# Where the loaded weights begin within a line of the on-chip memory: a two-layer transformer on one TensorE

## The chip, the cores and the metric

The kernel runs on one core of a Trainium2 chip. It has five engines that work side by side and wait for each other through semaphores: TensorE (PE in the profile; PEld is its weight load), VectorE (DVE), ScalarE (ACT), GpSimd (POOL) and SyncE (SP, which here issues the weight transfers). The metric is the device time of one launch in microseconds (us).

## What is computed

Two layers run one after the other on 256 tokens of width 2048. The first layer has a modulation (`adaln`), neighbourhood attention over 16 heads, and a feed-forward part with a short convolution. The second layer has 8 heads of a chunked recurrence (`mlstm`) and 16 heads of causal attention. The operations that matter here are the large products:

```python
q, k, v = split(h @ w_qkv)                          # 2048 x 6144
x = x + g1 * (attention(q, k, v) @ w_o)             # 2048 x 2048
gate, up = split(dwconv3(hf @ w_up))                # 2048 x 11008
x = x + g2 * ((silu(gate) * up) @ w_down)           # 5504 x 2048
proj = rms_norm(x) @ w_in_2                         # 2048 x 15440
y_a = (sigmoid(o_a) * h_a * silu(z_a)) @ w_a        # 2048 x 2048
y_b = (o_b * silu(z_b)) @ w_b                       # 2048 x 2048
out = x + (sigmoid(g_a) * y_a + sigmoid(g_b) * y_b) @ w_out
```

## The kernel before, in words

**Split numbers.** Each float32 operand of a product is split in two parts of a reduced type (float32r): `hi` holds the leading bits and `lo` the rest. A product is then hi·hi + hi·lo + lo·hi.

**Weights.** All weights are cut into units (`Unit`, line 179) and run in one fixed list. The planner in `run_units` (line 389) is plain Python that runs while the program is built: it keeps a clock of its own and writes each engine's instructions down in an order. SP brings a unit of 1 MB into a `raw` tile. `emit_prep` (line 343) splits each half of a unit: ACT casts `raw` into a `whi` tile and DVE subtracts to make a `wlo` tile, of 1024 columns each. There are five buffers of each.

**Two ways to multiply.** In `GemmX` (line 491) the activations are loaded into the array and the weights move through it. In `GemmW` (line 476) it is the other way round: 128 weight columns are loaded and held, and the activations move. There, the activations of one k-chunk stand side by side as 256 `hi` and 256 `lo` columns, so that one product with `whi` moves 512 columns and one with `wlo` moves the 256 `hi` columns. This is called a pair below: 512 columns, then 256, each with a weight load of its own. Every `GemmW` comes out of `pair_units` (line 1071). The profile names a product as out<-moving,loaded: `bank<-hf,whi` moves `hf` and has `whi` loaded.

**Which products are pairs.** The second half of the attention output (`o`), the whole feed-forward part (`hf`, `hid`), nearly all of the second layer's projections (`h2`, which the profile shows as `h`, since it leaves numbers out) and its three output products (`ya`, `ob`, `yp`).

**Addresses.** A tile of the program begins at a fixed byte in each partition of the on-chip memory. Lines 534 and 535 put in two small tiles (64 bytes on the left, 32 on the right) that do nothing but shift what comes after. As the program is laid out, `raw` begins at a multiple of 128 bytes, and `whi`, `wlo`, `h`, `o`, `hf`, `hid`, `h2`, `ya`, `ob`, `yp`, `latq` and `latkv` all begin 64 bytes past one. The steps within them (128 columns, 256, 512) are multiples of 128 bytes, so every weight load and every moving read of those tiles begins 64 bytes past a multiple of 128.

**The gate ring.** In the second layer's attention the gates `z` (16 tiles of 128x256, one a head) are computed ahead of the head that uses them: `mla_z` (line 1722) takes a buffer of `zring` (profile: `bz`) as soon as a gate's product is done, and `mla_attn` (line 1862) gives it back after the head's output has been multiplied by it (profile: `obF<-bank,bz`). The work list has two gates (heads 2g+2 and 2g+3), then the projections of heads 2g and 2g+1. If no buffer is idle, `need` (line 230) writes down pending steps of other heads, in the order of their due times, until one is. The main list stands still meanwhile, and PE runs its instructions in the order written.

**gone.** A small tile of 8x256 that `misc` (line 1417) uses once while it computes the recurrence's gates. The ring `E` (one buffer) is used by the recurrence's heads, which start after that.

Of the kernel before, what the change touches and what calls it, by code (L numbers as in the profile page):

```python
# [12 lines left out]
F32 = mybir.dt.float32  # L13
F32R = mybir.dt.float32r
# [96 lines left out]
class Bank:  # L111
    def __init__(self, owner, i):
        self.owner, self.i, self.busy, self.tfree = owner, i, False, 0.0
# [65 lines left out]
class Unit:  # L179
    def __init__(self, src, kt, cols, body=None, pre=None, post=None, raw=None):  # L180
        self.src, self.kt, self.cols = src, kt, cols
        self.body, self.pre, self.post, self.raw = body, pre, post, raw
        h = (kt + 1) // 2
        self.subs = [(0, h), (h, kt - h)] if kt > 1 else [(0, 1)]
        if raw is not None:
            self.subs = [(0, kt)]


class Kern:
# [153 lines left out]
    def emit_prep(self):  # L343
        u, s = self.preps[self.np]
        self.np += 1
        k0, nk = u.subs[s]
        self.ct = max(self.now, u.ready)
        if u.raw is not None:
            u.raw(u.view)
        else:  # L350
            n = nk * u.cols
            hi = self.p_w.tile([128, 1024], F32R, tag="whi", name="whi")
            lo = self.p_w.tile([128, 1024], F32R, tag="wlo", name="wlo")
            src = u.tile[:, k0 * u.cols:k0 * u.cols + n]
            self.A.copy(out=hi[:, 0:n], in_=src)
            self.nsplit += 1

            def rest():
                self.V.tensor_sub(out=lo[:, 0:n], in0=src, in1=hi[:, 0:n])
                u.parts[s] = tuple(x[:, 0:n].rearrange("p (k c) -> p k c", k=nk) for x in (hi, lo))  # L360
                u.at[s] = self.ct
                if s == len(u.subs) - 1:
                    self.next_dma(u)
            self.at(max(0.0, self.ct - self.now), rest)
            return
        self.next_dma(u)
# [161 lines left out]
class Model(Kern):  # L528
# [542 lines left out]
    def pair_units(self, w, K, c0, xs, evac, need=None, pre=None, nb=2, j0=0, nj=2):  # L1071

        us = []
        for p in range(0, nj, nb):
            def done(j, out, b, last, p=p):
                self.spawn(evac(j0 + p + j, out, b), 0.2 + 0.4 * j)
            g = GemmW(self, K, nb, xs, done, need)
            us += self.block_units(w, K, c0 + 128 * p, 128 * nb, g, kt=16 // nb)
        us[0].pre = pre
        return us  # L1080

# [232 lines left out]
    def c_begin(self):  # L1314
        sums = self.stats_sums()
        self.L.pop("hid")
        self.R.pop("x2")
        p = self.L.push("ya")
        self.sgring = Ring(self, p, "sga", [128, 256], F32, 8)
        self.ya = p.tile([128, KD, 512], F32R, name="ya")  # L1320
        self.yaH, self.yaL = self.ya[:, :, 0:256], self.ya[:, :, 256:512]
        p = self.R.push("cp")
        self.cg = {x: p.tile([128, 2, 64], F32, name="cg" + x) for x in "qk"}
        self.sg = {x: p.tile([128, 2, 64], F32, name="sg" + x) for x in "qk"}
        self.krt = p.tile([128, 2, 64], F32, name="krt")
        self.sskr = p.tile([128, 32], F32, name="sskr")[:, 0:2]
        r = self.r2 = p.tile([128, 256], F32, name="r2")
        self.r2c = p.tile([128, 32], F32, name="r2c")[:, 0:2]
        p = self.R.push("ml")
        self.p_ml = p  # L1330
        self.qring = Ring(self, p, "mq", [128, 2, 256], F32R, 3)
        self.kring = Ring(self, p, "mk", [128, 2, 256], F32R, 3)
        self.vring = Ring(self, p, "mv", [128, 2, 2, 288], F32R, 3)
        self.gring = Ring(self, p, "G", [128, 2, 256], F32, 3)
        self.cring = Ring(self, p, "mct", [128, 256], F32, 3)
        self.soring = Ring(self, p, "so", [128, 256], F32, 4)
        self.ering = Ring(self, p, "E", [128, 384], F32, 1)
        self.wring = Ring(self, p, "W", [128, 2, 384], F32R, 1)
        self.haring = Ring(self, p, "ha", [128, 256], F32, 2)
        self.tring = Ring(self, p, "T", [128, 512], F32, 1)  # L1340
        self.fring = Ring(self, p, "fold2", [128, 256], F32, 2)
        self.krx2 = p.tile([128, 256], F32, name="krx2")
        for nm in ("gi", "gz", "ga", "gb", "gc", "gone"):
            setattr(self, nm, p.tile([8, 256], F32, name=nm))
        self.acol = p.tile([128, 2, 8], F32, name="acol")
        self.fcol = p.tile([128, 2, 8], F32, name="fcol")
        for v in self.vring.tiles:
            for x in range(2):
                one = self.con("one") if x == 0 else self.con("tri0")[:, 0:1]
                self.V.tensor_copy(out=v[:, x, :, 256:258], in_=one.unsqueeze(1).to_broadcast([128, 2, 2]))  # L1350
        self.q, self.k, self.v, self.Gt = {}, {}, {}, {}
        self.qk_ready, self.mv_ready, self.G_ready, self.ya_ready = {}, {}, {}, set()
        self.gates_ready = self.kr_ready = self.rope_done = False
        self.c_ready = True
        yield from self.stats_end(D, sums, r, self.r2c)
        self.r_ready = True
        self.spawn(self.rope_tables(p), 1.0)
# [339 lines left out]
    def mla_begin(self):  # L1697
        self.need(lambda: self.y_stashed == 4)
        self.L.pop("ya")
        self.R.pop("y")  # L1700
        self.sgring = Ring(self, self.L.push("sgb"), "sgb", [128, 256], F32, 8)
        p = self.R.push("obf")
        self.obF = p.tile([128, KD, 256], F32, name="obF")
        p = self.R.push("mla")
        self.lat = {n: p.tile([128, 2, 4, 256], F32R, name="lat" + n) for n in ("q", "kv")}
        self.lat_ready = set()
        self.qring = Ring(self, p, "bq", [128, 2, 512], F32R, 2)
        self.kring = Ring(self, p, "bk", [128, 2, 512], F32R, 2)
        self.qrring = Ring(self, p, "bqr", [128, 2, 256], F32R, 2)
        self.krring = Ring(self, p, "bkr", [128, 2, 256], F32R, 2)  # L1710
        self.vring = Ring(self, p, "bv", [128, 2, 2, 256], F32R, 2)
        self.zring = Ring(self, p, "bz", [128, 256], F32, 6)
        self.sqring = Ring(self, p, "bsq", [128, 2, 2, 192], F32, 2)
        self.ktring = Ring(self, p, "bkt", [128, 768], F32, 1)
        self.xring = Ring(self, p, "bx", [128, 2, 2, 64], F32, 3)
        self.pring = Ring(self, p, "bp", [128, 384], F32, 2)
        self.ptring = Ring(self, p, "bpt", [128, 2, 384], F32R, 2)
        self.q, self.k, self.v, self.qr, self.kr, self.rq, self.zb = {}, {}, {}, {}, {}, {}, {}
        self.b_ready, self.ob_ready = {}, set()
        self.need(lambda: self.kr_ready)  # L1720
# [433 lines left out]
```

## Time and profile before

| | |
|---|---|
| three timed runs, us | 2603.92, 2609.01, 2610.87 (median 2609.01) |
| the profiled execution, us | 2611.98 |
| its span from first to last instruction, us | 2610.2 |
| PE busy | 2550.1 us, 98% of the span, 16038 products |
| PE weight loads busy | 2268.7 us, 87% |
| DVE, ACT, POOL busy | 71%, 54%, 9% |
| memory traffic | 522 MB, 200 GB/s |
| granted TensorE clock | 0.995 of full speed on average |

Products are pipelined, so the recorded duration of one (some 390 ns for 512 columns) is longer than the distance from its start to the next one's start. The rate is read from the starts. A row of the timeline gives start, duration, engine, line, operation, out<-in and count; the chain of waits gives start, duration and what ran, with the number of instructions.

### The profile page before, as it was taken

To read this page: it belongs to the slowest core of one execution; us is meant where nothing else is said; L and a number is where in the kernel's file an instruction comes from. 1 tells how busy PE (TensorE), PEld (TensorE's weight loads), DVE (VectorE), ACT (ScalarE), POOL (GpSimd) and SP (SyncE) were. 2 spreads that over 40 slices of the span, in tenths; PEclk is the share of its full clock that TensorE was granted. 3 is DMA by queue.
4 is the path that set the end of the run, shared out by engine and by line. 5 is a ranking of instruction groups with operands and counts; after the bars stand their busy time and mean duration, and the time that the engine had idled before them with its cause. 6 is when DMAs were issued, how large, how long until landed. Compare 5 with 4: busy or idle time off the path is not lost.

```text
span 2610.2 us, 40676 instructions
## 1 busy us (share of the span) xinstructions
PE 2550.1 (98%) x16038; PEld 2268.7 (87%) x16038; DVE 1844.4 (71%) x3027; ACT 1420.7 (54%) x2617; POOL 241.3 (9%) x263
## 2 busy tenths in 40 slices
PE   4999999999989999999999999999999999999999
PEld 2799999999978888888888888888888888888888
DVE  7987777677677888787555568677665576677664
ACT  5664444344555555555444456667554467775442
POOL 5421111111110000000000050000000000000000
PEclk9999999999999999999999999999999999999999
DMA  7876776676556666666566554554555553345553
GB/s 267 297 259 221 197 247 189 195 221 182 202 183 225 222 230 225 212 232 219 183 210 208 194 191 163 184 186 158 181 187 200 205 175 134 121 142 209 201 202 147
DMA packets 82543, 522.37 MB, mean 200 GB/s; under 512 B 9232, under 2 KB 15376, under 8 KB 23856
## 3 DMA queue, kind: packets, MB, share of 16 engines
q1 hardware_dynamic: 76656, 501.88, 54.1%
q0 software_dynamic: 5696, 17.90, 4.1%
q8 instruction: 126, 2.06, 0.3%
q14 instruction: 65, 0.53, 0.1%
HBM read 511.35 MB, written 8.39 MB: 199 GB/s over the span
## 4 chain that ended last, share of the span: by engine, by line
PE 94%; DVE 4%; ACT 1%; issue 1%; DMA 0%; SPq 0%; DVEq 0%; ACTq 0%
PE bank L256 91%; PE bank L265 2%; DVE wlo L151 2%; DVE hL L151 0%; ACT L149 0%; DMA nx<-in_ctxT_dram 0%; ACT whi L151 0%; SPq L707 0%; DVE hf L151 0%; DVE gb L151 0%; DVE mct L151 0%; DVE cc L151 0%; DVE adaC L151 0%; PE bank L608 0%; DVE acc L151 0%
## 5 line engine op out<-in xcount | busy, mean ns | idle before, releaser
L151 DVE TENSOR_TENSOR wlo<-raw,whi 128x1024 fp32r<-128x1024 f32 (+3 forms) x822 | 983.3, 1208 | 236.4 <-ACT whi L151 232.2
L151 ACT CAST whi<-raw 128x1024 fp32r<-128x1024 f32 (+3 forms) x822 | 830.5, 1021 | 422.4 <-PE bank L256 321.8
L256 PE MATMUL bank<-h,whi 128*128 128x512 f32 (+1 forms) x1696 | 593.9, 395 | 0.0
L256 PE MATMUL bank<-hf,whi 128*128 128x512 f32 x1376 | 485.0, 397 | 2.6 <-DVE hf L151 2.6
L256 PE MATMUL bank<-h,wlo 128*128 128x256 f32 x1680 | 470.7, 280 | 0.0
L256 PE MATMUL bank<-hf,wlo 128*128 128x256 f32 x1376 | 386.9, 281 | 0.0
L256 PEld LDWEIGHTS bank<-h,whi 128*128 128x128 f32 x1696 | 317.2, 188 | 71.9
L256 PE MATMUL bank<-whi,hH 128*128 128x256 f32 x1280 | 367.1, 287 | 0.0
L256 PE MATMUL bank<-whi,hL 128*128 128x256 f32 x1280 | 362.8, 283 | 2.2 <-DVE hL L151 2.2
L256 PE MATMUL bank<-wlo,hH 128*128 128x256 f32 x1280 | 362.8, 283 | 1.2 <-DVE wlo L151 1.2
L256 PEld LDWEIGHTS bank<-h,wlo 128*128 128x128 f32 x1680 | 317.4, 189 | 0.5 <-DVE wlo L151 0.3
L256 PEld LDWEIGHTS bank<-hf,whi 128*128 128x128 f32 x1376 | 259.0, 188 | 64.7 <-DVE hf L151 3.9
L256 PEld LDWEIGHTS bank<-hf,wlo 128*128 128x128 f32 x1376 | 261.1, 190 | 0.0
L256 PEld LDWEIGHTS bank<-whi,hL 128*128 128x128 f32 x1280 | 245.7, 192 | 2.5 <-DVE hL L151 2.4
L256 PEld LDWEIGHTS bank<-wlo,hH 128*128 128x128 f32 x1280 | 245.8, 192 | 2.3 <-DVE wlo L151 1.8
L256 PEld LDWEIGHTS bank<-whi,hH 128*128 128x128 f32 x1280 | 245.7, 192 | 1.0
L256 PE MATMUL bank<-hid,whi 128*128 128x512 f32 x688 | 243.1, 399 | 0.0
L256 PE MATMUL bank<-hid,wlo 128*128 128x256 f32 x688 | 193.2, 281 | 0.0
L151 DVE SCALAR_TENSOR_TENSOR acc<-raw,cs,acc 128x512 f32<-128x512 f32 x240 | 186.8, 778 | 6.8
L256 PEld LDWEIGHTS bank<-hid,whi 128*128 128x128 f32 x688 | 129.3, 188 | 32.2
L151 ACT COPY fold<-bank 128x256 f32<-128x256 f32 x118 | 43.6, 372 | 160.9 <-PE bank L256 158.2
L256 PEld LDWEIGHTS bank<-hid,wlo 128*128 128x128 f32 x688 | 130.0, 189 | 0.0
(334 smaller groups left out, 3695.7 us busy)
## 6 DMA issues: line engine op xcount, KB each, us to landing
raw<-in_w_in_dram SPq DMA_DIRECT2D x120, 1024.0 KB, 4.8
raw<-in_w_ada_dram SPq DMA_DIRECT2D x86, 1024.0 KB, 4.9
raw<-in_ffn_w_up_dram SPq DMA_DIRECT2D x86, 1024.0 KB, 4.9
raw<-in_na_w_qkv_dram SPq DMA_DIRECT2D x42, 1024.0 KB, 4.9
raw<-in_ffn_w_down_dram SPq DMA_DIRECT2D x40, 1024.0 KB, 4.9
raw<-in_na_w_o_dram SPq DMA_DIRECT2D x16, 1024.0 KB, 5.0
raw<-in_w_a_dram SPq DMA_DIRECT2D x16, 1024.0 KB, 5.0
raw<-in_w_b_dram SPq DMA_DIRECT2D x16, 1024.0 KB, 4.9
```

What stands on the lines that cost most here:

```text
L151: r = f(*a, **kw)
L256: self.T.matmul(out, lhsT, rhs, start=start, stop=stop)
L265: self.T.transpose(out, in_, self.con("id"))
```

## The change

A unit gets a flag `held`. `pair_units` sets it for all its units, that is, wherever weights are held and 512 columns move. The split tiles grow from 1024 to 1056 columns (128 bytes more, so that the next tile still begins 64 bytes past a multiple of 128), and a held unit uses columns 24 to 1047 of them. Those begin 96 bytes later: 32 bytes past a multiple of 128. Units that are not held use columns 0 to 1023 as before.

The ten split tiles take 1280 bytes a partition more. To make room, `gone` is no tile of its own but the corner of the tile `E0`, and `zring` has five buffers in place of six. Tiles after the split tiles move by 1280 bytes and those below the freed ones by 1024, both multiples of 128.

```diff
-        self.body, self.pre, self.post, self.raw = body, pre, post, raw
+        self.body, self.pre, self.post, self.raw, self.held = body, pre, post, raw, False
...
-            hi = self.p_w.tile([128, 1024], F32R, tag="whi", name="whi")
-            lo = self.p_w.tile([128, 1024], F32R, tag="wlo", name="wlo")
+            c = slice(24, 1048) if u.held else slice(0, 1024)
+            hi = self.p_w.tile([128, 1056], F32R, tag="whi", name="whi")[:, c]
+            lo = self.p_w.tile([128, 1056], F32R, tag="wlo", name="wlo")[:, c]
...
             us += self.block_units(w, K, c0 + 128 * p, 128 * nb, g, kt=16 // nb)
+        for u in us:
+            u.held = True
...
-        for nm in ("gi", "gz", "ga", "gb", "gc", "gone"):
+        for nm in ("gi", "gz", "ga", "gb", "gc"):
             setattr(self, nm, p.tile([8, 256], F32, name=nm))
+        self.gone = self.ering.tiles[0][0:8, 0:256]
...
-        self.zring = Ring(self, p, "bz", [128, 256], F32, 6)
+        self.zring = Ring(self, p, "bz", [128, 256], F32, 5)
```

## Rows read from the trace of the kernel before

**Rows 1.** The page: busy time, and the chain that ended last by engine and line.

```profile
PE 2550.1 (98%) x16038; PEld 2268.7 (87%) x16038; DVE 1844.4 (71%) x3027; ACT 1420.7 (54%) x2617; POOL 241.3 (9%) x263
PE 94%; DVE 4%; ACT 1%; issue 1%; DMA 0%; SPq 0%; DVEq 0%; ACTq 0%
```

**Rows 2.** The chain in order of time, the feed-forward stretch: start, us, what, products.

```profile
863.79 110.94 PE bank L256 x640
975.17 113.07 PE bank L256 x640
1088.67 110.94 PE bank L256 x640
```

**Rows 3.** Instructions on tiles hid and yp: duration min/median/max, first and last start.

```profile
L256 PE MATMUL bank<-hid,whi x688: 395/398/403, 1240.9 to 1483.6; 128*128 128x512 f32 x172
...
L256 PE MATMUL bank<-hid,wlo x688: 277/281/284, 1241.1 to 1483.9; 128*128 128x256 f32 x172
...
L256 PE MATMUL bank<-yp,whi x256: 395/398/403, 2515.8 to 2605.9; 128*128 128x512 f32 x128
```

**Rows 4.** Products by line and shape: the held pairs, counts and mean ns.

```profile
L256 PE MATMUL bank<-h,whi 128*128 128x512 f32 x1664 | 588.2, 397 | 0.0
L256 PE MATMUL bank<-hf,whi 128*128 128x512 f32 x1376 | 485.0, 397 | 2.6 <-DVE hf L151 2.6
L256 PE MATMUL bank<-hid,whi 128*128 128x512 f32 x688 | 243.1, 399 | 0.0
L256 PE MATMUL bank<-ob,whi 128*128 128x512 f32 x256 | 90.7, 399 | 0.0
L256 PE MATMUL bank<-ya,whi 128*128 128x512 f32 x256 | 90.6, 399 | 0.0
L256 PE MATMUL bank<-yp,whi 128*128 128x512 f32 x256 | 90.5, 399 | 0.0
...
L256 PE MATMUL bank<-o,whi 128*128 128x512 f32 x128 | 45.3, 399 | 0.0
```

**Rows 5.** Timeline of PE: 512 columns of weights move, activations loaded.

```profile
1540.11 0.39 PE L256 MATMUL bank<-wlo,h 128*128 128x512 f32 x1
1540.34 0.62 PE L256 MATMUL bank<-whi,h 128*128 128x512 f32 x2
1540.79 0.39 PE L256 MATMUL bank<-wlo,h 128*128 128x512 f32 x1
```

**Rows 6.** Timeline of PE: 256 columns move, only 4 columns loaded, nine products apart.

```profile
111.20 0.28 PE L256 MATMUL bank<-whi,cst 128*4 128x256 f32 x1
...
112.22 0.28 PE L256 MATMUL bank<-wlo,cst 128*4 128x256 f32 x1
```

**Rows 7.** Timeline of PE: 256 columns move, 128 columns loaded, three products apart.

```profile
500.04 0.28 PE L256 MATMUL bank<-whi,hL 128*128 128x256 f32 x1
...
500.40 0.28 PE L256 MATMUL bank<-whi,hL 128*128 128x256 f32 x1
```

**Rows 8.** Timeline of ACT: gate tiles taken in the second layer's attention.

```profile
2147.49 0.66 ACT L151 COPY bz<-bank 128x256 f32<-128x256 f32 x2
2177.32 0.37 ACT L151 COPY bz<-bank 128x256 f32<-128x256 f32 x1 [1.57 <-DVE obF L151]
```

**Rows 9.** Timeline of PE where heads' steps stand ahead of the main list.

```profile
2172.86 0.28 PE L256 MATMUL bank<-h,wlo 128*128 128x256 f32 x1
2172.97 0.82 PE L265 MATMUL bank<-cons,bkt 128*128 128x128 f32 x6
2173.63 0.82 PE L265 MATMUL bank<-cons,bp 128*128 128x128 f32 x6
2175.10 0.38 PE L256 MATMUL bank<-bpt,bv 128*128 128x256 f32 x1 [0.65 <-ACT bpt L151]
2176.04 0.79 PE L256 MATMUL bank<-bpt,bv 128*128 128x256 f32 x5 [0.56 <-DVE bpt L151]
...
2177.99 0.44 PE L256 MATMUL bank<-whi,latkv 128*128 128x512 f32 x1
```

**Rows 10.** Waits of the whole run: PE for the splits.

```profile
PE bank L256 <- DVE wlo L151: 20.4, 21, 3.3
```

## The prediction, made before the changed kernel ran

> **What bounds the kernel now.** I read the page first. PE is busy for 98% of the span and 94% of the chain that ended last is PE's own work [rows 1]. DVE, ACT and the transfers have room, so the time is the number of products times the distance between their starts. The reader is to see there that little can be gained except inside that distance.
>
> The second view is the chain in order of time, because it shows PE's undisturbed stretches with their counts. Three neighbouring ones each hold 640 products, which is 320 pairs of the same product with the same tile `hf`, and they last 110.94, 113.07 and 110.94 us [rows 2]. A pair thus takes 346.7 ns in two of them and 353.3 ns in the one between. No address changed from one to the next. The pair has two rhythms and falls into one or the other after an interruption. The third view is that of single tiles: `hid` runs 687 distances in 1483.6 - 1240.9 = 242.7 us and `yp` 255 in 90.1 us, both 353.3 ns a pair without exception [rows 3].
>
> The fourth view is the timeline, for what the two halves of a pair take in other company. When weights move and activations are loaded, three 512-column products take 1540.79 - 1540.11 = 0.68 us, 226.7 ns each, with 128 columns loaded each time [rows 5]. With only 4 columns to load, nine products of 256 columns take 112.22 - 111.20 = 1.02 us, 113.3 ns each [rows 6]. With 128 columns loaded the same size takes 0.36 us for three, 120 ns each [rows 7]. So a weight load beside a short product costs 6.7 ns, and nothing beside a 512-column one in that order. The best company gives 226.7 + 113.3 = 340.0 ns for a pair. Held pairs are 6.7 ns above this in the good rhythm and 13.3 ns in the slow one. That gap is what a shift of the loaded weights against the moving activations can reach.
>
> **The pairs and what is slow now.** The counts of the 512-column rows add up to 1664 + 1376 + 688 + 3 x 256 + 128 = 4624 pairs [rows 4]. Products of `hid`, `ob`, `ya`, `yp` and `o` have a mean of 399 ns [rows 4], that of the slow rhythm of `hid` and `yp` [rows 3]: 688 + 768 + 128 = 1584 slow pairs. Of the 1376 with `hf`, 640 lie in the two fast stretches [rows 2] and 736 are left. For the 1664 with `h` I take half, 832, since their mean of 397 is that of `hf` [rows 4], about half of which is slow. That makes 3152 slow pairs and 1472 fast ones.
>
> **The shift of the held weights.** Today the load and the moving read both begin 64 bytes past a multiple of 128. Afterwards the load begins 32 bytes past one and the moving read stays. In a load of 512 bytes the first boundary of 128 bytes then comes after 24 columns and no longer after 16. Nothing is added to PE's list: the count of loads and products, the columns and the order are the same. What may change is how a load and a moving read that run at the same time get in each other's way. That they do is shown by 120 against 113.3 ns [rows 6, 7], and that it hangs on their timing is shown by the two rhythms on one address [rows 2]. The trace has no load at another offset, so the price is bounded from both sides. At best the pair comes to 340.0 ns [rows 5, 6]. At worst every pair is like the longest one in the slow rhythm: its products last 403 and 284 ns where the medians are 398 and 281 [rows 3], 8 ns more, so 361 ns. I take the good rhythm, 346.7 ns, for every pair. It is the level nearest to the rows of the pair itself that a better meeting of the two reads has already been seen to give, and nothing in the trace shows a 512- and 256-column pair below it. This saves 113.07 - 110.94 = 2.13 us in 320 pairs, 6.66 ns a pair, for 3152 pairs: 21.0 us, all of it on the path.
>
> What the trace shows here speaks against a rule. The Trainium skill, "SBUF — State Buffer", section "Who interferes with whom", states that PE has two independent read ports, one for the moving operand and one for weight loads, and that only the port pair of VectorE and GpSimd causes contention. By that rule the place of the weights can't matter, and the sum would have no saving; the first rival below gives that time. The 6.7 ns between the rows with 4 and with 128 loaded columns speak against it. The page's "Specifications (TRN2)" name lines of 16 bytes; a shift by 32 bytes leaves the place within such a line as it was, which points the same way as the rule, and no row here shows such a line.
>
> **The splits.** ACT and DVE write their parts 96 bytes further on in the same number of instructions. PE waits for DVE's part for 20.4 us in 21 places of the whole run [rows 10]; for the rest the splits lie beside products. I put this edit at nothing. If writing at that offset were slower by a tenth, those 20.4 us would grow by about 2 us; if faster, they would shrink by as much.
>
> **The gate ring of five.** Two gates are copied into `bz` at 2147.49 us, and the next copy waits until 2177.32, released by the product that ends the first head [rows 8]. The six buffers are therefore all full there. With five, the sixth copy would already have to wait for that product, 29.8 us after its present place, and so in each later group: of the eight pairs of gates, the second gate of the third to the eighth, six places. The wait isn't idle time by itself. The planner writes down the pending steps of the heads until a buffer is free, so the heads' steps come earlier in PE's list and the main products, which cover their latency now, later. One place of today shows the price. After the last main product at 2172.86 come transposes and the heads' last products, and the next main product starts at 2177.99. PE stands for 0.65 us and then 0.56 us for ACT and DVE, and counted from starts the two products that wait come 0.82 us late each, 1.6 us in all [rows 9]. Queued behind them is the whole main list. Six places at 1.6 us are 10 us. Today's price is in part replaced, so it may be as little as 3 us; if the whole stretch of 5.0 us between two main products were lost each time, 30 us. I take 10, the measured place times the count.
>
> **The rest.** `gone` shares memory with a tile that is first used after it, so nobody waits. Moving tiles by 1280 and 1024 bytes keeps every distance to a multiple of 128. Both at nothing.
>
> **Sum.** On the profiled execution: 2611.98 - 21.0 + 10 = 2601 us, of which 1.8 us lie outside the span. The median of the runs lies 3.0 us lower, so 2598 us, 0.4% under the median of 2609.0. About 0.3%, 7.8 us, is what a measurement of this kernel can tell from no change: faster is below 2601.2, slower above 2616.8.
>
> **Rivals.**
> - *The shift does nothing.* The rhythms are chosen by when the stream starts, as on one address now [rows 2], and stay as mixed as they are. Then only the ring is left: 2609 + 10 = 2619 us, or 2612 with a ring at 3. Against it stand the 6.7 ns between rows 6 and 7.
> - *The load leaves the moving read in peace.* All pairs come to 340.0 ns: 3152 x 13.3 + 1472 x 6.7 = 51.8 us less, and 10 for the ring, 2567 us. For it speaks that 512 columns with a full load reach 226.7 ns today [rows 5], against it that 256 columns with a full load were never under 120 in a steady stream [rows 7].
> - *The new offset is the worse one* (slower). The load's boundaries then meet those of the moving read more often, and the place is every held pair. The pair goes to 353.3 ns for all (1472 x 6.66 = 9.8 us more) or to 361 (another 4624 x 8 = 37 us): 2609 + 10 + 10 = 2629 to 2666 us. It decides as soon as the pair's mean passes 351 ns, today's mix.
>
> **How the numbers follow.** Forecast 0.36, nothing 0.20, peace 0.24, worse 0.20. The forecast with a ring of 3 to 30 us spans 2591 to 2618; six parts in ten of it lie under 2601, the rest within 0.3% of the median. Peace is faster throughout. "Nothing" is within 0.3% when the ring costs under 8 us, a third of it, and else slower; worse is slower. That gives faster 0.22 + 0.24 = 0.46, same 0.14 + 0.07 = 0.21, slower 0.13 + 0.20 = 0.33. The range must hold both signs: from 2560 (peace with a cheap ring) to 2630 (nothing with a dear ring, worse at its mild end). Left out are the upper part of "worse" and single ends of the rest, under 0.2. The forecast's own range is 2591 to 2618.
>
> **What would show it.** Right: the chain's stretches with `hf` take 110.9 us for 640 products every time, `hid` and `yp` come to 346.7 ns from first to last start, with products of `hid` shorter than 395 ns. Peace would show 108.8 us for 640 products. Rhythms as now, mixed, would show the first rival; `hid` with 403 ns as its median the last. For the ring, the sixth copy into `bz` starts right after the first head's last product, and PE's idle rows between 2110 and 2385 us grow by single microseconds in six places; more would show as idle time in front of `bpt` products. The prediction is wrong if the pair has a level that the trace before doesn't have.

## The result and the profile after

The changed kernel takes 2640.2 us (median of four runs, 2639.0 to 2642.1) against 2609.4 us of the kernel before on the same chip: a ratio of 1.012, 95% interval 1.010 to 1.013. It is 31 us slower. The forecast was 2598 us, range 2560 to 2630. The profiled execution took 2642.1 us, its span is 2640.1 us.

The page of the kernel after, its busy line and the chain by engine, stands against [rows 1]:

```profile
PE 2563.4 (97%) x16038; PEld 2280.2 (86%) x16038; DVE 1847.1 (70%) x3027; ACT 1440.1 (55%) x2629; POOL 240.4 (9%) x263
PE 92%; DVE 4%; ACT 2%; issue 1%; DMA 0%; SPq 0%; DVEq 0%; ACTq 0%
```

PE does the same 16038 products, yet is busy for 13 us more, and its share of the chain falls from 94 to 92%. So the products themselves became slower somewhere, and PE stands longer too.

Where, the chain in order of time tells (start, us, what, products), against [rows 2]:

```profile
858.61 111.60 PE bank L256 x640
970.65 111.62 PE bank L256 x640
1082.71 111.60 PE bank L256 x640
```

The three stretches with `hf` are alike now, 111.6 us or 348.8 ns a pair, a value that no stretch before had. They lie between the two rhythms of [rows 2]: better than their mixture, worse than the good one. They also begin earlier, at 858.6 in place of 863.8 us. Up to here the change gains.

The loss sits in the second layer's attention. The same stretch of the trace, kernel after first, then the kernel before (us; busy time and count of PE, PEld, DVE, ACT and POOL; granted clock; DMA share; GB/s):

```profile
2140.00:2385.00 245.00, 225.65 (x1162) 193.15 (x1161) 146.11 (x371) 170.32 (x412) 7.83 (x14) 0.87 0.31 110
```

```profile
2140.00:2385.00 245.00, 242.61 (x1412) 213.25 (x1411) 173.14 (x428) 175.65 (x447) 8.07 (x14) 0.99 0.39 138
```

Where the kernel before gets through 1412 products, the one after gets through 1162. PE stands for 19 us in place of 2, and the granted clock is 0.87 in place of 0.99. The waits of PE from 2100 to 2400 us say for whom it stands (us in total, times, longest):

```profile
PE bank L265 <- DVE bp L151: 10.7, 12, 1.5
PE bank L256 <- ACT bq L151: 4.6, 6, 0.9
PE bank L256 <- DVE bq L151: 2.5, 6, 0.5
```

Six times, twelve heads: the six places that the prediction counted. The timeline of PE shows the first of them (start, us, engine, line, operation, count, idle time before it), where [rows 9] showed the kernel before:

```profile
2140.83 0.44 PE L256 MATMUL bank<-bk,bq 128*128 128x128 f32 x2 [0.67 <-ACT bq L151]
2141.62 0.33 PE L256 MATMUL bank<-bk,bq 128*128 128x128 f32 x1 [0.35 <-DVE bq L151]
...
2144.41 0.89 PE L256 MATMUL bank<-bk,bq 128*128 128x256 f32 x3
...
2147.77 0.87 PE L265 MATMUL bank<-cons,bp 128*128 128x128 f32 x3 [1.53 <-DVE bp L151]
2148.89 0.87 PE L265 MATMUL bank<-cons,bp 128*128 128x128 f32 x3 [0.25 <-DVE bp L151]
2149.42 1.71 PE L256 MATMUL bank<-bpt,bv 128*128 128x256 f32 x6
2150.93 0.73 PE L256 MATMUL bank<-whi,latkv 128*128 128x512 f32 x1
2151.46 0.63 PE L256 MATMUL bank<-wlo,latkv 128*128 128x512 f32 x1
...
2155.08 0.39 PE L256 MATMUL bank<-wlo,latkv 128*128 128x512 f32 x1
```

Between 2139.12 and 2150.93 no main product stands. Scores (products of `bk` with `bq` and of `bkr` with `bqr`), transposes and products of two heads follow each other, 36 in a row on PE's list after six transposes for the queries; three of the six places have six transposes of keys more. Four of these steps wait for ACT or DVE. From 2144.41 on the products are longer: 0.63 us for a product of 512 columns at 2151.46, 0.39 us for the same at 2155.08. The granted clock shows why (three windows of the kernel after, columns as above):

```profile
2139.00:2143.90 4.90, 3.88 (x24) 2.92 (x22) 2.42 (x7) 3.77 (x5) 0.00 (x0) 1.00 0.61 214
2145.00:2150.00 5.00, 3.21 (x13) 2.20 (x13) 2.81 (x11) 2.10 (x9) 0.00 (x0) 0.50 0.00 0
...
2155.50:2160.00 4.50, 4.50 (x24) 4.06 (x23) 3.38 (x7) 3.72 (x12) 0.00 (x0) 1.00 0.14 25
```

It goes from full speed, 2.4 GHz, to half, 1.2 GHz, for some ten microseconds, and back.

The sixth copy of a gate starts at 2151.62, released by the first head's last step, as forecast from [rows 8] (timeline of ACT):

```profile
2138.23 0.38 ACT L151 COPY bz<-bank 128x256 f32<-128x256 f32 x1
2151.62 0.37 ACT L151 COPY bz<-bank 128x256 f32<-128x256 f32 x1 [1.34 <-DVE obF L151]
```

### The profile page after: what moved, and what is told of

The parts are those of the page before. It is cut to its first block, busy times and chain, and to the rows that moved or that the text cites. A ratio compares the mean times of both kernels' runs of the same rounds, so it can differ in the third digit from the quotient of the medians.

```text
span 2640.1 us, 40705 instructions
## 1 busy us (share of the span) xinstructions
PE 2563.4 (97%) x16038; PEld 2280.2 (86%) x16038; DVE 1847.1 (70%) x3027; ACT 1440.1 (55%) x2629; POOL 240.4 (9%) x263
## 4 chain that ended last, share of the span: by engine, by line
PE 92%; DVE 4%; ACT 2%; issue 1%; DMA 0%; SPq 0%; DVEq 0%; ACTq 0%
PE bank L256 90%; PE bank L265 2%; DVE wlo L151 2%; ACT L149 0%; ACT whi L151 0%; DVE hL L151 0%; DMA nx<-in_ctxT_dram 0%; SPq L709 0%; ACT bp L151 0%; DVE bank L151 0%; DVE hf L151 0%; DVE cc L151 0%; DVE gb L151 0%; DVE bq L151 0%; DVE mct L151 0%
## 5 line engine op out<-in xcount | busy, mean ns | idle before, releaser
L256 PEld LDWEIGHTS bank<-whi,hL 128*128 128x128 f32 x1280 | 242.7, 190 | 2.5 <-DVE hL L151 2.4
L256 PEld LDWEIGHTS bank<-wlo,hH 128*128 128x128 f32 x1280 | 242.7, 190 | 2.4 <-DVE wlo L151 1.8
L256 PEld LDWEIGHTS bank<-whi,hH 128*128 128x128 f32 x1280 | 242.7, 190 | 0.9
```

The lines of the kernel that those rows point to most:

```text
L256: self.T.matmul(out, lhsT, rhs, start=start, stop=stop)
```

## The experiments

### Which part of the change did it

The first four runs take the change apart. The missing gate buffer can be put back without moving anything, since an accumulator tile has had its last use by then:

```diff
         self.zring = Ring(self, p, "bz", [128, 256], F32, 5)
+        self.zring.put(len(self.zring.tiles))
+        self.zring.tiles.append(self.accring.tiles[0][:, 0:256])
```

> The changed kernel with a sixth gate buffer put back; it takes the memory of an accumulator that has had its last use by then, so nothing else moves. Theory (the ring of five is the whole loss, the shift of the held weights a gain of 4566 to 4624 pairs x 2.45 ns = 11 us): 2609 - 11 = 2598 us, TensorE clock 1.00 from 2140 us to the last stage, and the six episodes with 1.2 GHz gone. Rival (the shifted or longer weight tiles, or the moved tiles, slow the second attention): about 2640 us as now, episodes still there. Rival (the shift gains nothing and the ring lost only 31): 2609 us.

Measured: 2600.3 us, ratio 0.997 (0.996 to 0.998). The clock and the waits of the kernel before are back (window from 2140 to 2385 us of this run):

```profile
2140.00:2385.00 245.00, 242.60 (x1404) 213.73 (x1403) 173.37 (x424) 176.51 (x446) 9.81 (x17) 0.99 0.39 140
```

The counterpart is the kernel before with the ring alone:

```diff
-        self.zring = Ring(self, p, "bz", [128, 256], F32, 6)
+        self.zring = Ring(self, p, "bz", [128, 256], F32, 5)
```

> The kernel before with five gate buffers in place of six and nothing else changed. Theory (the ring alone loses the time in the second attention): 2609 + 31 + 11 = about 2651 us, with the granted clock at about 0.88 between 2140 and 2390 us. Forecast on record for the ring: 2609 + 10 = 2619 us. Rival (the weight tiles are the cause): 2609 us, clock 1.00.

Measured: 2650.0 us, ratio 1.017 (1.015 to 1.018). So the ring costs 2650.0 - 2607.8 = 42 us by itself, and 2640.2 - 2600.3 = 40 us on top of the rest of the change. That rest gains 7.5 us. The ring is the loss.

How the 40 us divide follows from the busy times: PE is busy for 2563.4 us after and 2539.0 us with six buffers, 24.4 us more for the same products. The pairs are not the cause, 1623.1 and 1623.9 us by their starts. What is left is the low clock. The spans differ by 2640.1 - 2598.3 = 41.8 us, so 17.4 us are standing.

Two more runs ask whether even six are too few, with seven buffers in the changed kernel and in the kernel before (one more line as above).

> The changed kernel with seven gate buffers, the two further ones in the halves of that accumulator. If the number of waits for a gate buffer sets the loss, then the places that still wait with six (three folds) become fewer: each cost about 1.6 us in the kernel before, so 2 to 5 us under the run with six and the shift, 2593 to 2596 us. If six already hide everything, the same as with six: 2598 us.

> The kernel before with a seventh gate buffer, without the shift. With three waiting places at 1.6 us to be saved: 2604 to 2607 us. If six already hide them: 2609 us. The difference to the shifted kernel with seven is again the shift alone: 11 us by the pairs, 0 if the shift does nothing.

Measured: 2600.6 and 2613.3 us (ratios 0.997 and 1.002). No gain: with seven PE's waits on `bpt` even go from 1.3 to 2.7 us in all. Six buffers hide what there is to hide. The difference of the two, 12.7 us, is the rest of the change once more, 5 us larger than above; kernels with the old buffers vary that much, as the last section shows.

### Why the ring costs 42 us and not 10

Two causes are possible for the slow clock: that PE stands, or that the heads' products stand in a row. The first test fills the standing with products that nobody needs (they go into a bank that is overwritten next):

```diff
+    def fill(self, b, h, n):
+        if h % 2 == 0 and h < 12:
+            v = self.v[h // 2][0]
+            for _ in range(n):
+                self.T.matmul(b.t, v[:, 0, 0, 0:128], v[:, 0].rearrange("p t c -> p (t c)"), start=True, stop=True)
...
         b = self.bank()
+        self.fill(b, h, 6)
         for c in range(3):
             self.tr(b.t[:, col(c)], p[:, col(c)])
```

> The changed kernel with its five gate buffers; in each of the six episodes eight products of 512 columns that nobody needs are put into PE's list where PE stands: two ahead of the first head's scores, six ahead of its transposes of `bp`. They take 8 x 0.227 = 1.8 us an episode of the 3 us that PE stands there. PE's busy time after exceeds that with six buffers by 2563.4 - 2539.0 = 24.4 us, which is the products at 1.2 GHz; the rest of the 42 us is standing. If the fall of the clock follows from the standing, it stays away here: about 24 us less, 2616 us. If it comes with the heads' own products, the clock falls as now and the fillers hide or add: 2640 to 2651 us.

Measured: 2633.3 us, neither the one nor the other: 7 us under the changed kernel, where the first theory had 24. The stage, the first episode's slow window, and its timeline, all of this run:

```profile
2140.00:2385.00 245.00, 238.58 (x1258) 202.74 (x1259) 153.47 (x386) 173.77 (x418) 7.82 (x14) 0.93 0.33 118
...
2144.00:2150.00 6.00, 5.99 (x18) 4.46 (x19) 3.25 (x12) 2.03 (x8) 0.00 (x0) 0.51 0.00 0
```

```profile
2143.00 0.93 PE L256 MATMUL bank<-bk,bq 128*128 128x256 f32 x3
2143.86 1.01 PE L256 MATMUL bank<-bkr,bqr 64*128 64x256 f32 x3
2144.80 2.93 PE L1871 MATMUL bank<-bv 128*128 128x512 f32 x6
...
2150.32 0.45 PE L256 MATMUL bank<-whi,latkv 128*128 128x512 f32 x1
2150.61 0.39 PE L256 MATMUL bank<-wlo,latkv 128*128 128x512 f32 x1
```

The waits on `bp` are gone, and the clock still falls at the same place of the list, during the second head's scores: the fillers themselves take 2.93 us for six, and PE is busy for 5.99 of 6.00 us at a clock of 0.51. But it rises 7.6 us after its fall (2143.00 to 2150.61) in place of 10.7 us (2144.41 to 2155.08). So the standing on `bp` isn't what lets the clock fall. It prolongs the fall: over the whole stage the clock is 0.93 in place of 0.87.

The kernel before shows a fall as well, one in this stage, with no standing ahead of it (two windows and the timeline of PE, kernel before):

```profile
2270.00:2274.80 4.80, 4.80 (x30) 4.07 (x28) 1.49 (x5) 4.24 (x9) 0.00 (x0) 1.00 0.52 195
2274.80:2278.20 3.40, 3.40 (x12) 3.18 (x12) 2.28 (x13) 1.91 (x10) 0.00 (x0) 0.50 0.00 0
```

```profile
2274.20 0.62 PE L256 MATMUL bank<-bk,bq 128*128 128x256 f32 x3
2274.75 0.95 PE L256 MATMUL bank<-bkr,bqr 64*128 64x256 f32 x3
2275.63 0.69 PE L256 MATMUL bank<-whi,latq 128*128 128x384 f32 x1
```

PE is busy for 4.80 of 4.80 us ahead of it, and the fall comes near the end of the scores of two heads, 24 products in a row, as it does in the changed kernel. But main products follow at once, at 2275.63, and the clock is back before 2279. In the changed kernel the next main product comes at 2150.93, more than six microseconds after the fall. That this makes the difference between a short fall and a long one fits the traces, that of the fillers too; no run has tested it alone.

The second test takes the row of head products apart while five buffers stay. A gate without a free buffer waits in the planner, and main products are written down meanwhile:

```diff
         def evac(j, halves, b):
+            while not self.zring.idle:
+                yield 0.3
             t, i = yield from self.fold(halves, b, self.zring)
```

> The changed kernel with its five gate buffers; a gate for which no buffer is free waits in the planner and lets main products be written down, in place of having the heads' steps written down at once. Of the six runs of 36 head products in a row on PE's list two are left, the other heads stand between main products in runs of at most 24, as with six buffers. Theory (the price sits in such a run: 42 / 6 = 7 us each, standing and slow clock together): 2600 + 2 x 7 = 2614 us, clock below 1.00 in two stretches between 2140 and 2385 us. Rival (fewer buffers cost by themselves, wherever the heads stand): 2630 to 2640 us.

Measured: 2613.6 us, 0.4 us from what was expected. The long falls of that run are where the two rows of 36 are left, in the first two windows. Where the heads stand between main products one short fall is left, in the fourth window, right behind twelve products of scores:

```profile
2140.00:2175.00 35.00, 32.20 (x162) 27.48 (x161) 19.92 (x51) 23.55 (x56) 1.12 (x2) 0.85 0.35 113
2175.00:2210.00 35.00, 31.86 (x163) 27.27 (x162) 20.93 (x53) 24.67 (x59) 1.12 (x2) 0.85 0.27 86
2210.00:2240.00 30.00, 29.98 (x175) 26.07 (x173) 18.63 (x50) 21.47 (x57) 1.28 (x2) 1.00 0.36 129
2240.00:2270.00 30.00, 29.08 (x160) 25.28 (x161) 21.11 (x55) 22.91 (x56) 1.13 (x2) 0.94 0.39 132
```

So it isn't the number of buffers that costs. It is a row of 36 head products on PE's list, 7 us each, some 3 us of it standing and 4 us slow clock.

### What the shift does

With the ring out of the way the rest gains 7.5 us, where 21 had been forecast. The rest is two edits: weights 32 bytes past a multiple of 128, and tiles of 4224 in place of 4096 bytes, which puts the buffers 4224 bytes apart. Three runs keep the longer tiles and six buffers and vary the offset of the held weights:

```diff
-            c = slice(24, 1048) if u.held else slice(0, 1024)
+            c = slice(0, 1024)        # 64; slice(16, 1040): 0; slice(8, 1032): 96
```

> As the run with the shift and six gate buffers, but the held weights begin at the start of their longer tiles, which is 64 bytes past a multiple of 128 as in the kernel before. If the place of the weights against the multiples of 128 makes the rhythm, the two fixed rhythms of 346.7 and 353.3 ns a pair come back, and the time lies where the kernel before lies, 2601 to 2615 us. If the longer tile (4224 in place of 4096 bytes) makes it, the uniform 348.8 ns stays and the time is 2600 us.

> Held weights at a multiple of 128 bytes, activations stay 64 past one, six gate buffers. If what counts is that load and moving read begin at different places within 128 bytes, the uniform rhythm of 348.8 ns a pair stays, 2600 us. If the place itself counts, a third rhythm may show: 340.0 ns would be 4566 x 8.8 = 40 us less than with 348.8 (2560 us), 353.3 ns for all 21 us more (2621 us). If the half of 128 (64 bytes) counts as the same place, the two fixed rhythms come back, 2601 to 2615 us.

> Held weights 96 bytes past a multiple of 128, activations stay 64 past one, six gate buffers; the distance between the two is 32 bytes as in the changed kernel, with the other sign. If the distance alone counts, 348.8 ns a pair and 2600 us. If the sign counts, another rhythm: 346.7 ns for all would be 10 us less (2590 us), 353.3 ns for all 21 us more (2621 us).

Measured: 2599.3, 2611.6 and 2609.1 us (ratios 0.996, 1.001 and 1.000). The first is the surprise: without any shift the longer tile alone gives the 2600 us. The chain's stretches with `hf` in that run:

```profile
857.81 111.63 PE bank L256 x640
969.88 111.64 PE bank L256 x640
1081.96 111.64 PE bank L256 x640
```

It could still be that tiles behind the longer ones moved. The next run has tiles of 4096 bytes and a gap of 1280 bytes behind them:

> As the run with longer tiles, weights at their start and six gate buffers (2599 us), but the split tiles are 4096 bytes again and a gap of 1280 bytes behind them keeps every later tile at its place. Only the distance from one weight buffer to the next differs. Theory (formed after that run): the distance of 4224 bytes, not the 32 bytes, made the rhythm; the two fixed rhythms of 346.7 and 353.3 ns a pair come back, 2601 to 2615 us. Rival (the moved activation tiles made it): mixed rhythm of 349 ns, 2599 us.

Measured: 2607.3 us, ratio 1.000, with 110.94, 113.06 and 110.94 us in the stretches: the two rhythms of [rows 2] are back. So the distance of 4224 bytes makes the uniform 348.8 ns. The other half of the change, the 32 bytes at the old distance, is a change of one pad:

```diff
-        ...tile_pool(name="shiftl", bufs=1, side="left")).tile([128, 16], F32, name="shiftl")
+        ...tile_pool(name="shiftl", bufs=1, side="left")).tile([128, 8], F32, name="shiftl")
         self.p_w = self.es.enter_context(tc.tile_pool(name="w", bufs=self.SUB, side="left"))
+        ...tile_pool(name="shiftm", bufs=1, side="left")).tile([128, 8], F32, name="shiftm")
```

> The kernel before with all weight tiles moved by 32 bytes, so that they begin 32 bytes past a multiple of 128 at their old distance of 4096 bytes; everything else is at its old place, six gate buffers. Theory (the distance between buffers counts): the rhythms stay fixed over whole stretches, and the 32 bytes by themselves give no steady gain: 2601 to 2615 us with 346.7 and 353.3 ns. Rival (the 32 bytes count, as the forecast had it): one level for all pairs, 346.7 ns is 2611.98 - 21 = 2591 us, 340.0 ns is 2560 us; a new level on the other side, 353.3 ns or more, 2621 us or more.

Measured: 2590.3 us, ratio 0.994 (0.993 to 0.996), next to the 2591 us of the rival that follows the forecast. The chain's stretches of this run, and its products on tile `hid` against [rows 3]:

```profile
855.54 110.94 PE bank L256 x640
966.91 110.94 PE bank L256 x640
1078.29 110.93 PE bank L256 x640
```

```profile
L256 PE MATMUL bank<-hid,whi x688: 390/390/390, 1229.7 to 1467.9; 128*128 128x512 f32 x172
```

Every pair takes 346.7 ns there and every product with `whi` 390 ns: 238.2 us for 687 distances in place of 242.7. From start to start, 4623 pairs of the run (the last one has no successor) take 1617.5 us in place of 1634.7, 17.1 us less. The spans differ by 20.1 us, 2610.2 - 2590.1. This run moves the weights that aren't held too: the first pair begins at 694.5 us in place of 700.0.

### Is 32 a special place, and why does 4224 spoil it

Four more runs keep buffers 4096 apart: the whole pool 128 bytes further on; `wlo` alone 128 bytes further on; the pool at 0; the pool at 96 (pads of other sizes, as above; in all but the third the tiles behind the pool move by 128 bytes and the sixth gate buffer lies in the accumulator tile).

> The kernel before with all weight tiles 32 bytes past a multiple of 128 at their old distance of 4096 bytes, as in the run with 2590 us, but 128 bytes further on (288 in place of 160 past a multiple of 512; the tiles behind them move by 128 bytes). Theory A (the place within 128 bytes sets the level, an even distance between buffers lets it hold): 346.7 ns for every pair and 2590 us. Theory B (the place within 512 bytes counts, and buffers 4224 apart are uneven because they go through four such places): another level, anywhere from 340 (2560 us) to 353.3 ns (2620 us).

> As the run with the weight tiles 32 bytes past a multiple of 128 and 4096 apart (2590 us), but the five tiles `wlo` lie 128 bytes further on, so that `whi` and `wlo` of a pair are not at the same place within 512 bytes, the same for every pair. Theory C (what spoils the rhythm at a distance of 4224 is that `whi` and `wlo` of a pair lie unevenly to each other): not 346.7 ns for all, 349 ns and about 2600 us. Theory D (what spoils it is the change from buffer to buffer): 346.7 ns stays, 2590 us.

> The kernel before with all weight tiles at a multiple of 128 bytes, 4096 apart, all else in place. With tiles 4224 apart this offset gave 351.6 ns a pair against 348.8 at 32. If the offset orders the levels in the same way here: above 346.7, at most 353.3 ns for all, 2600 to 2620 us. If any offset other than the activations' own 64 gives the good rhythm: 346.7 ns, 2590 us. If none of it can be told from another offset: 340.0 ns would be 2560 us.

> The kernel before with all weight tiles 96 bytes past a multiple of 128, 4096 apart (tiles behind them move by 128 bytes). With tiles 4224 apart this offset gave 350.8 ns. In the same order as there: between the levels at 32 and at 0, so about 350 ns, 2600 to 2615 us. If any offset other than the activations' own 64 gives the good rhythm: 346.7 ns, 2590 us.

Measured: 2589.6, 2590.9, 2606.2 and 2605.2 us (ratios 0.993, 0.993, 0.999 and 0.999). In the first two the stretches stay at 110.94 and 110.95 us, so theories A and D held and B and C fell there (in the second the 128 pairs with `o` alone ran at 350.0 ns). At 96 they are 113.06, 113.07 and 110.94 us. At 0 all three are the slow ones, 113.05 us (chain of that run, the first of them):

```profile
846.94 113.05 PE bank L256 x640
```

As with the longer tiles 0 is the worst. Here 32 alone is the best; there 32 and 64 were alike. Yet the run at 0 isn't slower than the kernel before, because its stretches begin 17 us earlier, at 846.94 in place of 863.79 us. The first stage gains: the weights move and 128 columns of `hL` and `hH` are loaded, the case of [rows 7]. 216 such products took 25.91 us twice in the kernel before. At 32 they take 25.57 and 25.56 us, at 96 25.65 and 25.35, and at 0 (the same chain):

```profile
217.88 24.58 PE bank L256 x216
285.44 25.44 PE bank L256 x216
```

Two last questions: does the shift work if only the held weights are moved, as the change does it, and do the best places of different products add up? For that five slots of 4096 bytes lie in one long tile:

```diff
-            hi = self.p_w.tile([128, 1024], F32R, tag="whi", name="whi")
-            lo = self.p_w.tile([128, 1024], F32R, tag="wlo", name="wlo")
+            o = 1024 * (self.nsplit % self.SUB) + (24 if u.held else 0)
+            hi, lo = self.whi[:, o:o + 1024], self.wlo[:, o:o + 1024]
```

The second run differs by 8 in place of 24 and a pad. In both the slots of the two kinds overlap by 96 and 32 bytes, so where held and other weights alternate some columns of a weight are changed before they are used; instructions, sizes and order are those of the kernel before.

> The change's shift alone: held weights 32 bytes past a multiple of 128, all other weights at 64 as before, buffers 4096 bytes apart (five slots in one long tile each for `whi` and `wlo`, so that a held part can begin 96 bytes into its slot), six gate buffers. Theory (the level is set by the place of the weights of the pair, and holds because the slots lie evenly): 346.7 ns for every held pair. In the run with all weights at 32 the held pairs took 1634.7 - 1617.5 = 17.1 us less than in the kernel before: 2609 - 17 = 2592 us. Rival (that gain needed all weights at 32): 349 ns or mixed, 2600 to 2610 us.

> As the run with held weights at 32, but all other weights at a multiple of 128 in place of 64. In the run with every weight at 0 the 3 x 1280 products of 256 columns with `hL` and `hH` came 5.47 + 5.35 + 5.11 = 15.9 us sooner, those with `o` 1.0, and 384 of 512 columns with `h` and `latkv` 2.3 us later. Theory (each kind of product has its own best place and they add up): 2592 - 15.9 - 1.0 + 2.3 = 2577 us, with the first held pairs starting at about 683 us. Rival (the gains don't add, since a stage that ends sooner waits for its transfers): about 2590 us.

Measured: 2604.7 us (ratio 1.000) and 2590.6 us (0.994). Both miss the theory by 13 us and come out at the times that their rivals had. The first shows three rhythms in one run, 346.7 and 350.0 ns in its chain's stretches with `hf` (the third takes 112.00 us too) and 353.3 ns in its products with `hid`:

```profile
854.67 110.95 PE bank L256 x640
966.05 112.00 PE bank L256 x640
```

```profile
L256 PE MATMUL bank<-hid,whi x688: 397/397/397, 1231.8 to 1474.5; 128*128 128x512 f32 x172
```

In that run the held `whi` lie 288 and the held `wlo` 416 bytes past a multiple of 512, in the second 160 and 288, where the pairs hold 346.7 ns. There the first stage missed its gain (25.47 and 25.45 us for the 216 products), with `wlo` 128 bytes apart from `whi`. So 32 past a multiple of 128 isn't enough. The two runs differ in the place of `whi` and `wlo` within 512 bytes and in the offset of the other weights, and no run tells these apart; the pairs with `hid` run one after the other without any other weights, so the place is the likelier cause. The last run makes `whi` and `wlo` alike and switches the offset once, when the first held weights come:

```diff
+            self.off = 8 if u.held else self.off
+            o = 1024 * (self.nsplit % self.SUB) + self.off
...
+        self.whi = self.p_w.tile([128, 1024 * self.SUB + 128], F32R, name="whi")
+        self.wlo = self.p_w.tile([128, 1024 * self.SUB + 8], F32R, name="wlo")
```

> Slots 4096 bytes apart for `whi` and `wlo` in one long tile each, both at the same place within 512 bytes; the weights of the first stage (up to the first held pair) at a multiple of 128, from then on all weights 32 bytes past one; six gate buffers. Theory (the level hangs on the place within 128 bytes if `whi` and `wlo` lie alike, and each kind of product has its own best place): held pairs at 346.7 ns throughout as with all weights at 32 (2590 us), and the 3 x 1280 products with `hL` and `hH` at about 116 ns as with all weights at 0, which started the held pairs at 683 in place of 694 us: 2590 - 11 = 2579 us. Rival (those gains don't add): 2590 us, held pairs starting at 692 us or later.

Measured: 2577.0 us (2575.1 to 2579.7), ratio 0.988 (0.986 to 0.989), the fastest of all. In its chain the first stage has the times of the run at 0, the pairs those of the run at 32, so the two gains add:

```profile
218.33 24.58 PE bank L256 x216
285.88 25.44 PE bank L256 x216
...
844.97 110.94 PE bank L256 x640
956.34 110.95 PE bank L256 x640
1067.73 110.94 PE bank L256 x640
```

All of it by offset (the middle one of the three stretches with `hf`; 110.94 is 346.7 ns a pair, 113.07 is 353.3):

| bytes past a multiple of 128 | 4096 apart, all weights moved: us, stretch | 4224 apart, held weights moved: us, stretch |
|---|---|---|
| 0 | 2606.2, 113.05 | 2611.6, 112.52 |
| 32 | 2590.3, 110.94 | 2600.3, 111.61 |
| 64 | 2607.3 to 2609.4, 110.94 or 113.07 | 2599.3, 111.64 |
| 96 | 2605.2, 113.07 | 2609.1, 112.25 |

## Why the prediction was wrong, step by step

**What bounds the kernel.** Right in the main: what the runs gained and lost lies in the distance between PE's starts, which the clock sets too, and in the time that PE stands for a head's chain.

**The gate ring: the step that failed.** The six places were right, and so were the release of the sixth copy and the order (heads' steps earlier, main products later). The price per place was mis-sized: 1.6 us forecast, 7 us measured, 42 in place of 10 and above the upper bound of 30. [Rows 9] shows a place where 30 transposes and products of heads stand between two main products (it shows eighteen of them), with two stalls and without any scores. With five buffers 42 or 48 stand in a row, the scores of two heads among them, and their chain on ACT and DVE runs without cover from its first step. That is the standing, 17 us. The other part, 24 us of low clock, had no term at all. The kernel before had such a fall in that very stage, at 2274.8 us, and the prediction didn't look for it, nor ask what longer rows of head products would do to it. Its bound from above took the five microseconds between two main products as the worst that could be lost; after, two main products are nearly twelve apart.

**The shift of the held weights.** Right where all weights lie 32 bytes past a multiple of 128 at their old distance: 346.7 ns for every pair, with the 110.9 us a stretch and the products under 395 ns that the prediction named as its signs. The sum took 21.0 us for the pairs; they gave 17.1 there and 1634.7 - 1614.5 = 20.2 in the last run. That the time meets 2591 us so closely is in part luck, since that run gains with the other weights too. And offset 32 does not give that rhythm by itself: with the held weights alone moved it came in one run (`whi` and `wlo` at 160 and 288) and not in the other (288 and 416, 2604.7 us). "Peace" (340 ns) was seen in no stretch, and "worse" was seen at 0, not at 32. By the rule of the Trainium skill that was weighed ("SBUF — State Buffer", "Who interferes with whom": moving and loaded operand have ports of their own) the place could not matter; 2590.3 against 2607.8 us for 32 bytes speaks against that reading.

**The longer tiles: the second step that failed.** The prediction had no term for the distance from buffer to buffer. It put the moves of tiles at nothing, because every distance stays a multiple of 128, which was argued from the very boundary whose role was unknown. A distance of 4224 bytes carries the buffers through different places within 512 bytes, and the pair comes to 348.8 ns at offset 32 as at offset 64. By the pairs it took back 6.4 of the 17.1 us (1623.9 us with six buffers against 1617.5); the medians, 2600.3 and 2590.3, lie 10 us apart. The prediction named as its refutation that the pair has a level which the trace before doesn't have, and that is what the chain after showed. In the changed kernel the five buffers give pairs with `whi` and `wlo` at 288 and 416 (two of the five), 160 and 288, 32 and 32, and 416 and 160 past a multiple of 512. Its trace tells them apart, since the products run in the program's order: the distances of the pairs with `hid` have a mean of 350.1 ns at 288 and 416 (277 pairs), 349.5 at 160 and 288, 346.8 at 32 and 32, and 348.1 at 416 and 160 (136 to 138 pairs each), 348.9 over all. So the level goes with the buffer. It isn't a plain mixture of what each place gives when it is held throughout: 160 and 288 gave 346.7 ns there, and 288 and 416 gave 346.7 to 353.3. Why the place matters, and what the change from place to place adds, was not settled.

**The splits, `gone`, the moved tiles.** Right: PE's wait for `wlo` is 20.5 us in 21 places after, [rows 10] has 20.4 in 21. The run with moved tiles alone takes the time of the kernel before.

**The sum and the rivals.** 2611.98 - 11.6 (pairs by their starts, 1623.1 in place of 1634.7) + 42 = 2642.4 us; the profiled execution took 2642.1. That it meets so closely is luck, since the first stage's gain is not in it: the first pair begins at 696.6 us in place of 700.0. Of the rivals "the new offset is the worse one" had the measured time in its span, 2629 to 2666 us, but by luck: the pairs became faster, not slower. "The shift does nothing" had 2619 us with the same ring at 10. All rivals dealt with the shift, and none let the ring decide, though the upper bound of 30 was already larger than the whole gain.

## What to carry over

Before a buffer is taken from a ring, ask which instructions the scheduler will then write in a row, and price the whole row on PE's list with no main product beside it: its chain on the other engines and the clock that PE falls to. A single short fall of the clock in the trace before is a reason to ask what a longer row of the same products would do. Where a loaded and a moving operand stream together, try the start of the weights in steps of 32 bytes, for each kind of product by itself, and keep all buffers of a ring at the same place within 512 bytes; a pad of 32 bytes gave 0.6% here, two offsets together 1.2%. An edit that pays for another edit's memory is a change of its own and needs its own term.

## What the runs showed of the hardware

- The rhythm of a pair has fixed levels where all buffers lie alike. 640 products took 110.94, 112.00 or 113.07 us, 346.7, 350.0 or 353.3 ns a pair, steps of 3.3 ns. At one address the stream falls into one or another: the kernel with five buffers and no other edit ran its three stretches with 113.07, 110.94 and 113.07 us, the kernel before with 110.94, 113.07 and 110.94. The pairs of these two traces take 1623.5 and 1634.7 us. This is probably why the runs of the kernel before spread over 19 us (2596.4 to 2615.4) and those at 32 over some 5.
- Where the buffers lie unlike each other, the distance of a pair changes from buffer to buffer: 346.8 to 350.1 ns among the pairs with `hid` of the changed kernel.
- The place that is best depends on which operand holds the weights. With weights loaded and activations moving, 32 was the best and 0 the worst of four; with weights moving, 0 was the best and 64 the worst (the 216 products above).
- The granted clock fell to 1.2 GHz while PE was at work. In the kernel before PE was busy for 4.80 of 4.80 us ahead of the fall. In the run with fillers PE stood for only 0.20 and 0.35 us between its fillers and the fall, which came during the scores, products of 128 and 256 columns in rows of three; and it stayed down while PE was busy for 5.99 of 6.00 us. What of these products lets it fall was not tested.
